# Feed-forward input tiles moved apart in a hybrid encoder layer: untouched tiles of 8 to 120 numbers between them

## The chip, the cores and the metric

The kernel runs on one core of a Trainium2 chip. The metric is the device time of one execution in microseconds. The engines are named as in the profile: PE is TensorE, DVE is VectorE, ACT is ScalarE, POOL is GpSimd, SP is the engine that issues most DMAs.

## The reference

One layer of an encoder, for two sequences of 1024 rows and width 1024 (`x_prompt` and `x_sample`), each with its own conditioning vector `c`. All numbers are float32.

```python
mod = jax.nn.silu(c) @ w_ada + b_ada                 # shift, scale, gate, twice
h = rmsnorm(x, g_mix) * (1.0 + sc1) + sh1
z = h @ w_in
y_mla = mla_group(q_lat, kv_lat, k_pe, ...)          # latent attention, 4 heads, softmax over 1024 keys
y_four = fourier_group(f_in, w_four)                 # 2-D Fourier mixing in 8 groups of 64
x = x + ga1 * (jnp.concatenate([y_mla, y_four], axis=-1) @ w_out)
h2 = rmsnorm(x, g_ffn) * (1.0 + sc2) + sh2
ffn = (jax.nn.silu(h2 @ w_gate) * (h2 @ w_up)) @ w_down      # inner width 2816
y = rmsnorm(x + ga2 * ffn, g_final)
```

## The kernel before

**Precision.** Each product of two float32 matrices is made of three matmuls. `split` (L63 to L65) cuts a tile into a high part (a cast by ACT, L64) and a low part (source minus high part, usually by DVE, L65). `mm3` (L79 to L82) then multiplies high by high (L80), high by low (L81) and low by high (L82) into the same PSUM bank. In `nc.tensor.matmul(out, weights, moving)` the first operand is loaded into the array 128 columns at a time (a weight load, PEld in the profile), and the second streams through, here mostly 512 columns of 4 bytes. While a matmul streams, the weights of the next are being loaded.

**Stages.** Projections and Fourier mixing come first, then attention, from about 300 to 715 us (`scores`, L1211 to L1223: per head and half of 256 rows five matmuls of 512 columns for each half of the keys; sequence 0 up to 505 us, then sequence 1), then from about 746 us the feed-forward part: gate/up of sequence 0, its down projection, gate/up of sequence 1, its down projection.

**Feed-forward, gate/up.** Both gate/up products use a scheme of the Strassen kind with seven products in place of eight, so the normalised input `h2` of a sequence is kept as seven combinations, numbered k = 0 to 6. Each is a pair of tiles: `Hk0` holds the high part and `Hk1` the low part, both `[128, 4, 512]` float32, 8192 bytes in each partition. `prep_h` loads and splits them. For each of 22 blocks of the inner width, seven weight combinations are split by `hl` into a pair `wh`, `wl` of `[128, 512]` tiles (eight buffers each), and `prod` runs, for chunk c of four:

```python
mm3(ps, wh[:, cs], wl[:, cs], H[k][0][:, c, :], H[k][1][:, c, :], first and c == 0, c == 3, not first)
```

So `wh` and `wl` are the weights here, an H tile is what streams, and `Hk0` streams twice where `Hk1` streams once.

**Down projection.** `prod2` multiplies `wh`, `wl` by `wh`, `wl`: both operands are from the same eight-buffer tiles. Its raw data arrives in X0 and X1. Only in the last product of sequence 1 do H tiles serve again, as holders of both operands (`held`, filled by `prep_last`).

**Memory.** Tiles come from stacked pools. Pool `p5` (`w`) takes its tiles from one end of the on-chip memory; the loop over 16 tags in front of `prep_h` reserves X0, X1 and the fourteen H tiles one behind the other by calling `quad(tag)`. Pool `p5b` (`w5`), with `wh`, `wl`, the 18 `val` buffers and some more, grows from the other end (`side="right"`), next to an unused tile of 104 numbers, `edge`, made at the start. Memory that a pool takes over from an earlier one is guarded by waits, tile by tile (`reuse_waits="tile"`): the first writer of a tile waits for the last users of whatever lay there.

**Order.** Instructions stand on each engine in the order in which the code records them, with small corrections by `issue_after` and `first`. Nothing in that order depends on addresses; only waits do.

Of the kernel before, what the change touches and what calls it, by code (L numbers as in the profile page):

```python
# [12 lines left out]
F32 = mybir.dt.float32  # L13
# [8 lines left out]
P = 128  # L22
# [32 lines left out]
def hybrid_encoder_kernel(ctx: ExitStack, tc: tile.TileContext, a: dict):  # L55
# [111 lines left out]
    with ExitStack() as st:  # L167
        p1b = st.enter_context(ExitStack())
        w2 = p1b.enter_context(tc.tile_pool(name="p1b", bufs=1, side="right", reuse_waits="tile"))
        w = st.enter_context(tc.tile_pool(name="p1", bufs=1, reuse_waits="tile"))  # L170
# [747 lines left out]
    with ExitStack() as st:  # L918
        early = st.enter_context(ExitStack())
        wa = early.enter_context(tc.tile_pool(name="p2a", bufs=1, reuse_waits="tile"))  # L920
        w = st.enter_context(tc.tile_pool(name="p2", bufs=1, side="right", reuse_waits="tile"))
# [283 lines left out]
    with ExitStack() as st:  # L1205
        w = st.enter_context(tc.tile_pool(name="p3", bufs=1, side="right", reuse_waits="tile"))
# [158 lines left out]
    with ExitStack() as st:  # L1365
        w = st.enter_context(tc.tile_pool(name="p5", bufs=1, reuse_waits="tile"))
# [6 lines left out]
        def quad(tag, dt=F32):  # L1373
            return w.tile([P, 4, 512], dt, tag=tag, name=tag, bufs=1)


        for tag in ("H20", "X0", "X1", "H21", "H30", "H31", "H00", "H41", "H01", "H50", "H51", "H10", "H11", "H40", "H60", "H61"):
            quad(tag)

        def prep_h(H, s, n):  # L1380
# [611 lines left out]
```

## Time and profile before

| | us |
|---|---|
| median of two runs | 2029.03 (2029.02 to 2029.04) |
| the profiled execution | 2027.96 |
| its span, first to last instruction | 2026.1 |
| PE busy in the span | 1978.9 |
| DVE, ACT, POOL busy | 1399.9, 891.0, 827.2 |

How such rows are read. A row of the groups names the line, the engine, the operation, the tiles (out<-in, buffer numbers left out), the shape and the count, then the busy time in us and the mean of one in ns, then the idle time ahead of them and what ended it. All H tiles are one name, `H`, there. A row of a source line gives the least, median and greatest duration, and the first and last start. A row of the timeline gives the start and the duration in us. Matmuls overlap: a duration of 389 ns with starts 227 ns apart is a full stream, and the distance of starts is what a matmul costs. A row of the stretches gives the busy time and, in brackets, the number of instructions of PE, PEld, DVE, ACT and POOL (only those that are there), then the granted clock of PE, the DMA share and GB/s.

### The profile page before, as it was taken

The numbers are of one execution on the slowest core, as the hardware profiler recorded it, in microseconds if no ns is written. First come the engines' busy times: TensorE is split into PE (matmuls) and PEld (weight loads), VectorE is DVE, ScalarE is ACT, GpSimd is POOL, SyncE is SP. The second block draws the span as 40 slices with busy tenths as digits, with TensorE's granted clock in tenths as the row PEclk, the third lists the DMA queues.
The fourth block names the chain that finished last, engine by engine and source line by source line (L and its number), as shares of the span: only waits on it lengthen the run. The fifth ranks groups of instructions, "written<-read, shape, count | busy, mean of one in ns | idle before, by whom it ended". The sixth has DMA issues, their size and how long they took to land.

```text
span 2026.1 us, 28369 instructions
## 1 busy us (share of the span) xinstructions
PE 1978.9 (98%) x9910; PEld 1640.5 (81%) x9910; DVE 1399.9 (69%) x2076; ACT 891.0 (44%) x1732; POOL 827.2 (41%) x972
## 2 busy tenths in 40 slices
PE   6899999999999999999999999999999999999998
PEld 3788778888888878888888888877888888888876
DVE  4567758666677779777777676778755655667685
ACT  2675435555565564333333365454333333336441
POOL 0664212111313237879779410333554454410142
PEclk9999999999999999999999999999999999999999
DMA  9696884434544475645645587665322322358662
GB/s 392 256 324 205 287 312 109 134 94 101 151 119 140 142 259 181 212 163 190 205 158 196 177 309 246 214 233 177 124 95 104 111 98 104 109 186 276 220 229 94
DMA packets 183037, 376.64 MB, mean 186 GB/s; under 512 B 17997, under 2 KB 57549, under 8 KB 179053
## 3 DMA queue, kind: packets, MB, share of 16 engines
q1 hardware_dynamic: 165548, 321.33, 46.3%
q0 software_dynamic: 17344, 53.49, 8.9%
q8 instruction: 78, 1.28, 0.3%
q14 instruction: 67, 0.54, 0.1%
HBM read 262.75 MB, written 120.39 MB: 189 GB/s over the span
## 4 chain that ended last, share of the span: by engine, by line
PE 54%; DVE 4%; DMA 2%; issue 1%; POOL 1%; ACT 1%; SPq 0%; DVEq 0%; ACTq 0%; POOLq 0%
PE bank L81 18%; PE bank L80 18%; PE bank L82 18%; DVE wl L65 2%; DVE val L140 1%; DMA draw<-s_d 1%; DMA draw<-t_d 1%; DVE val L1789 0%; ACT wh L64 0%; DVE val L137 0%; DMA X<-hc_d 0%; POOL val L140 0%; POOL rs_y L108 0%; DVE val L1778 0%; DVE val L1763 0%
## 5 line engine op out<-in xcount | busy, mean ns | idle before, releaser
L80 PE MATMUL bank<-H,wh 128*128 128x512 f32 x1232 | 480.0, 390 | 3.3 <-DVE val L140 1.3
L81 PE MATMUL bank<-H,wh 128*128 128x512 f32 x1232 | 479.5, 389 | 0.3 <-DVE H L65 0.3
L82 PE MATMUL bank<-H,wl 128*128 128x512 f32 x1232 | 479.3, 389 | 0.2 <-DVE wl L65 0.2
L80 PEld LDWEIGHTS bank<-H,wh 128*128 128x128 f32 x1232 | 231.2, 188 | 54.1 <-DVE val L1669 2.2
L82 PEld LDWEIGHTS bank<-H,wl 128*128 128x128 f32 x1232 | 231.2, 188 | 48.5 <-DVE wl L65 0.5
L81 PEld LDWEIGHTS bank<-H,wh 128*128 128x128 f32 x1232 | 231.2, 188 | 48.3 <-DVE H L65 0.6
L65 DVE TENSOR_TENSOR wl<-draw,wh 128x512 fp32r<-128x512 f32 x286 | 202.9, 744 | 85.2 <-ACT wh L64 84.4
L140 DVE TENSOR_TENSOR val<-bank,val 128x512 f32<-128x512 f32 x200 | 136.6, 689 | 154.0 <-PE bank L82 151.9
L64 ACT CAST wh<-draw 128x512 fp32r<-128x512 f32 x286 | 168.3, 620 | 157.8 <-PE bank L81 90.3
L140 POOL TENSOR_TENSOR val<-val 128x512 f32<-128x512 f32 x58 | 83.1, 1441 | 353.1 <-DVE val L1763 189.6
L81 PE MATMUL bank<-wl,wh 128*128 128x512 f32 x572 | 223.7, 391 | 3.4 <-DVE wl L65 3.4
L82 PE MATMUL bank<-wh,wl 128*128 128x512 f32 x572 | 222.7, 389 | 0.0
L80 PE MATMUL bank<-wh 128*128 128x512 f32 x572 | 222.6, 389 | 0.0
L64 ACT CAST wh<-rgu 128x512 fp32r<-128x512 f32 x172 | 107.1, 623 | 258.3 <-PE bank L81 201.0
L64 ACT CAST wh<-val 128x512 fp32r<-128x512 f32 x133 | 82.3, 622 | 259.0 <-PE bank L81 244.0
L65 DVE TENSOR_TENSOR wl<-rgu,wh 128x512 fp32r<-128x512 f32 x172 | 171.0, 994 | 3.8 <-ACT wh L64 3.8
L65 DVE TENSOR_TENSOR wl<-val,wh 128x512 fp32r<-128x512 f32 x133 | 126.1, 950 | 64.4 <-ACT wh L64 64.3
L137 POOL TENSOR_TENSOR val<-rgu 128x512 f32<-128x512 f32 x80 | 112.7, 1409 | 92.9 <-DMA rgu<-in_wgu_dram 89.2
L81 PEld LDWEIGHTS bank<-wl,wh 128*128 128x128 f32 x572 | 107.3, 188 | 28.7 <-DVE wl L65 6.7
L80 PEld LDWEIGHTS bank<-wh 128*128 128x128 f32 x572 | 107.4, 188 | 22.5
L82 PEld LDWEIGHTS bank<-wh,wl 128*128 128x128 f32 x572 | 107.4, 188 | 22.1
L1228 DVE TENSOR_REDUCE mx<-ps_s 128x1 f32<-128x1024 f32 x64 | 78.2, 1221 | 60.6 <-PE ps_s L1223 60.2
(385 smaller groups left out, 4052.4 us busy)
## 6 DMA issues: line engine op xcount, KB each, us to landing
rgu<-in_wgu_dram SPq DMA_DIRECT2D x86, 512.0 KB, 4.3
draw<-s_d SPq DMA_DIRECT2D x143, 256.0 KB, 3.8
s_d<-val POOLq DMA_DIRECT2D x88, 256.0 KB, 4.1
draw<-t_d SPq DMA_DIRECT2D x88, 256.0 KB, 4.2
s_d<-val SPq DMA_DIRECT2D x66, 256.0 KB, 2.6
draw<-in_w_down_dram SPq DMA_DIRECT2D x55, 256.0 KB, 4.6
wada<-in_w_ada_dram SPq DMA_DIRECT2D x11, 1024.0 KB, 10.5
xt<-in_x_dram SPq DMA_DIRECT2D x16, 512.0 KB, 10.2
```

The source lines that it names most:

```text
L64: here["a"] = nc.scalar.copy(hi, src).ins
L65: here["v"] = (eng or nc.vector).tensor_tensor(out=lo, in0=src, in1=rd(hi), op=ALU.subtract).ins
L80: nc.tensor.matmul(out, lh, rh, start=first, stop=False, skip_group_check=cont)
L81: nc.tensor.matmul(out, lh, rl, start=False, stop=False, skip_group_check=cont)
L82: here["t"] = nc.tensor.matmul(out, ll, rh, start=False, stop=last, skip_group_check=cont).ins
L137: return eng.tensor_tensor(out=out, in0=x, in1=y, op=ALU.subtract).ins
L140: eng.tensor_tensor(out=out, in0=x, in1=y, op=ALU.add)
L1228: nc.vector.tensor_reduce(out=mx, in_=ps, axis=AX.X, op=ALU.max)
```

## The change

Ahead of ten of the sixteen tiles an extra tile is reserved that nothing writes or reads. Its size is 8 to 120 float32 numbers in each partition.

```diff
+        apart = {"H20": 64, "H21": 64, "H30": 96, "H00": 72, "H41": 48, "H01": 80, "H50": 8, "H10": 16, "H40": 24, "H60": 120}
         for tag in ("H20", "X0", "X1", "H21", "H30", "H31", "H00", "H41", "H01", "H50", "H51", "H10", "H11", "H40", "H60", "H61"):
+            if tag in apart:
+                w.tile([P, apart[tag]], F32, name=f"apart{tag}")
             quad(tag)
```

The extra tiles take 592 numbers, 2368 bytes, in each partition. Every H tile and X0, X1 start later than before, by 256 to 2368 bytes. `wh`, `wl` and the rest of `p5b` stay where they were. In the two built programs these are the addresses; all `wh` and `wl` buffers start at 64 modulo 512, and a weight chunk of 128 columns is 512 bytes long:

| tiles | modulo 512 before | modulo 512 after | distance to `wh`, `wl` before | after |
|---|---|---|---|---|
| H00, H01 | 64 | 224 | 0 | 160 |
| H10, H11 | 64 | 320 | 0 | 256 |
| H20 | 64 | 320 | 0 | 256 |
| H21 | 64 | 64 | 0 | 0 |
| H30, H31 | 64 | 448 | 0 | 384 |
| H40, H41 | 64 | 416 | 0 | 352 |
| H50, H51 | 64 | 256 | 0 | 192 |
| H60, H61 | 64 | 384 | 0 | 320 |
| X0, X1 | 64 | 320 | 0 | 256 |

The instructions of all engines stay the same, in the same order. Some waits at the start of the pool differ, as a moved tile covers other memory of the stage before. On ACT this is the place where the last split of the attention output (`o0b`) is followed by the first splits of an H pair, H00 from its raw data in H20. A bracket names the counters that an instruction waits for: DMAHW and DMASW count transfers issued by SP and POOL, the others an engine's instructions. Before:

```order
L64 COPY pt_8112<-ppt 128x4x128 [waits PE_49] x2
L64 COPY o0b_7948<-gb 128x256 [waits PE_49]
L64 COPY H_8313<-H_8293 128x1024 [waits DMAHW1_49]
L64 COPY H_8313<-H_8293 128x1024 [waits DMAHW2_49]
L1175 ACTIVATE xn,ms_8198<-x_7977 128x1024 [waits DMAHW7_49,DVE_49]
```

After (lines behind the change stand three further down; the numbers in the names differ since more tiles are made ahead of them):

```order
L64 COPY pt_8112<-ppt 128x4x128 [waits PE_49] x2
L64 COPY o0b_7948<-gb 128x256 [waits PE_49]
L64 COPY H_8323<-H_8303 128x1024 [waits DMAHW4_49,DMAHW5_49,DMAHW3_49,DMAHW7_49,DMAHW1_49,Pool_49]
L64 COPY H_8323<-H_8303 128x1024 [waits DMAHW2_49]
L1175 ACTIVATE xn,ms_8198<-x_7977 128x1024 [waits DMAHW7_49,DVE_49]
```

The first split of H00 now waits, besides for its own data, for four earlier loads and for POOL: H00 has come to lie partly on tiles `hca` and `hcb` of the stage before. The DVE split behind it waited for that POOL instruction before the change too. The other differences of this kind are the loads of H21 and H30 on SP, and on ACT the second use of L1448, which writes into H41.

## The prediction

> **What bounds the kernel now.** First the page: its span, the share of TensorE, and the chain that ended last.
>
> ```profile
> span 2026.1 us, 28369 instructions
> PE 1978.9 (98%) x9910; PEld 1640.5 (81%) x9910; DVE 1399.9 (69%) x2076; ACT 891.0 (44%) x1732; POOL 827.2 (41%) x972
> PE 54%; DVE 4%; DMA 2%; issue 1%; POOL 1%; ACT 1%; SPq 0%; DVEq 0%; ACTq 0%; POOLq 0%
> PE bank L81 18%; PE bank L80 18%; PE bank L82 18%; DVE wl L65 2%; DVE val L140 1%; DMA draw<-s_d 1%; DMA draw<-t_d 1%; DVE val L1789 0%; ACT wh L64 0%; DVE val L137 0%; DMA X<-hc_d 0%; POOL val L140 0%; POOL rs_y L108 0%; DVE val L1778 0%; DVE val L1763 0%
> ```
>
> TensorE works in 98% of the span, and 54% of the span lies in the three lines of mm3 (L80 to L82). So I ask next how many of those matmuls read the tiles that the change moves (groups by line), and how densely they follow each other (the stretches, first for the instructions of H alone, then for all engines).
>
> ```profile
> L80 PE MATMUL bank<-H,wh 128*128 128x512 f32 x1232 | 480.0, 390 | 3.3 <-DVE val L140 1.3 <-DVE val L1669 0.8 <-ACT H L64 0.7
> L81 PE MATMUL bank<-H,wh 128*128 128x512 f32 x1232 | 479.5, 389 | 0.3 <-DVE H L65 0.3
> L82 PE MATMUL bank<-H,wl 128*128 128x512 f32 x1232 | 479.3, 389 | 0.2 <-DVE wl L65 0.2
> ...
> 1330.00:1806.00 476.00, 419.68 (x1848) 346.70 (x1848) 0.00 (x0) 0.53 (x1) 1.00 0.36 124
> ...
> 1320.00:1805.00 485.00, 481.32 (x2117) 396.41 (x2115) 314.16 (x405) 168.01 (x294) 219.04 (x216) 1.00 0.36 127
> ```
>
> 3 x 1232 = 3696 matmuls stream an H tile, 528 for each of the seven pairs. In the second gate/up stage 1848 of them fill 419.68 us, that is 227.1 ns from one start to the next, at a granted clock of 1.00. In that stretch TensorE is idle for 3.7 us of 485, while VectorE works for 314 us. **Whatever a matmul there takes longer, the kernel takes longer**; the other engines have slack.
>
> **What the change does to instructions.** It adds none, removes none and leaves their order on every engine as it was: the new tiles are never written or read. It does two things: it moves addresses, and with them a few waits for earlier users of the memory.
>
> **The waits.** The first ACT split of H00 now also waits for the POOL subtraction into hcb, four loads into hca and its own data; its old wait was the data alone. The second L1448 waits for the four hc_d stores as well. On SP the load of H21 waits for a later split of qa, the load of H30 for one matmul more.
>
> ```profile
> 692.20 1.62 POOL L137 TENSOR_TENSOR hcb<-hca,hcb 128x512 f32<-128x512 f32 x1
> 694.12 0.57 POOL L1282 DMA_DIRECT2D hc_d<-hcb  x1 [0.30 <-POOL hcb L137]
> ...
> L1282 POOL DMA_DIRECT2D hc_d<-hcb x4: 571/614/682, 622.4 to 694.1; - x4
> ...
> DMA to landing us min/median/max: 4.2/7.8/10.4
> ...
> 721.71 2.00 ACT L64 CAST H<-H 128x1024 fp32r<-128x1024 f32 x2
> ...
> 704.68 0.41 DVE L65 TENSOR_TENSOR qa<-gb,qa 128x256 fp32r<-128x256 f32 x1
> ...
> 715.29 0.98 SPq L1395 DMA_DIRECT2D H<-hc_d  x2
> ```
>
> The POOL operation ends at 693.8 us, the loads that it read are older, and the last store lands by 694.1 + 10.4 = 704.5 us. ACT starts that split at 721.71 and the second L1448 comes later still. The last qa split ends at 705.1, and SP issues the load at 715.29. Every new wait is over 10 us old when it is reached, except the single matmul, 0.23 us, in front of the H30 load; behind it on SP stand loads for splits some 10 us later. I take **0 us**, with 0 to 0.3 as ends. Were this cover gone, a split 10 us late would cost TensorE about that.
>
> **The addresses.** That is the real question: does a matmul care where its streamed tile lies against the weights being loaded beside it? Before, every H tile, wh and wl lie at 64 bytes modulo 512, so the distance is 0. After, it is 160 (H00, H01), 256 (H10, H11), 256 and 0 (H20, H21), 384 (H3x), 352 (H4x), 192 (H5x), 320 (H6x). The trace of before has a natural experiment on this. In attention, scores() runs the same five matmuls of 512 columns for both sequences; in the program as built the lat tiles of sequence 0 lie at 64 modulo 512, as qa and qp do (distance 0), those of sequence 1 at 0 (distance 448). Line L1222, first up to 505 us (sequence 0), then after (sequence 1), and one stretch of each from the timeline:
>
> ```profile
> L1222 PE MATMUL ps_s<-lat,qp x64: 389/389/400, 301.7 to 501.9; 128*128 128x512 f32 x64
> ...
> L1222 PE MATMUL ps_s<-lat,qp x64: 388/394/398, 505.5 to 713.2; 128*128 128x512 f32 x64
> ...
> 301.69 0.39 PE L1222 MATMUL ps_s<-lat,qp 128*128 128x512 f32 x1
> 303.96 0.39 PE L1222 MATMUL ps_s<-lat,qp 128*128 128x512 f32 x1
> ...
> 521.34 0.39 PE L1219 MATMUL ps_s<-lat,qa 128*128 128x512 f32 x1
> 523.66 0.28 PE L80 MATMUL gb<-wq_h,ql 128*128 128x256 f32 x1
> ```
>
> The median is 389 ns at distance 0 and 394 at 448. Ten matmuls from 301.69 to 303.96 make 227 ns each; ten from 521.34 to 523.66 make 232. **A distance of 448 costs 5 ns.** The Fourier output stage gives other distances at 512 columns: six matmuls on wm and B (distance 64), then six on wm and A (a mix of 32, 352, 416 and 480):
>
> ```profile
> 275.52 0.39 PE L80 MATMUL bank<-wm,B 128*128 128x512 f32 x1
> 276.91 0.39 PE L80 MATMUL bank<-wm,A 128*128 128x512 f32 x1
> 278.29 0.39 PE L1033 MATMUL bank<-wn,ny 128*128 128x512 f32 x1
> ```
>
> 1.39 us over six is 231.7 ns, 1.38 over six 230.0: 4.7 and 3.0 more than 227. Between this and the scores row I take 5 ns, since that row has the most samples in a steady stream, with 3.0 and 5.3 as ends.
>
> [...]
>
> Distance 256 has no steady row at 512 columns. The nearest are the 448-column matmuls on wz, three at 256 and then three at 0:
>
> ```profile
> 103.29 0.36 PE L80 MATMUL bank<-wz_h,eoh 128*128 128x448 f32 x1
> 103.90 0.36 PE L80 MATMUL bank<-wz_h,eoh 128*128 128x448 f32 x1
> 104.50 0.37 PE L80 MATMUL bank<-wz_h,eoh 128*128 128x448 f32 x1
> ```
>
> 203 ns against 200, so I take 3 ns for 256, with 0 (if the pattern repeats every 256 bytes) and 5.3 as ends.
>
> **The sum.** Five pairs at distances other than 0 and 256: 5 x 528 x 5 ns = 13.2 us. At 256 stand the whole pair H10/H11 (528) and two thirds of H20/H21 (352, as mm3 streams the first of a pair twice): 880 x 3 ns = 2.6 us. The 176 on H21 stay at 0. Together 15.8 us, all on TensorE and not hidden. Ends: 2640 x 3.0 = 7.9, and 3520 x 5.3 = 18.7. A slower TensorE may let the waits of 3.7 us a stage shrink; I count nothing for that. X0 and X1 move as well, but TensorE does not read them; their readers ACT, DVE and POOL work beside it. If VectorE lost its slack there, its L65 would have to slow by half first (485 over 314).
>
> The profiled execution took 2027.96 us, 1.9 more than its span and 1.07 less than the median of 2029.03. With 15.8 it would be 2043.8; against the median, **2045 us, 0.8% longer**.
>
> **Rivals.** *Distance does not matter.* What sequence 1 shows would then be due to its neighbours. For it speaks that some matmuls at distance 0 in attention also come slowly: three on wv and o0b from 729.57, then three more.
>
> ```profile
> 729.57 0.40 PE L80 MATMUL gb<-wv,o0b 128*128 128x512 f32 x1
> 730.28 0.39 PE L80 MATMUL gb<-wv,o0b 128*128 128x512 f32 x1
> 730.97 0.39 PE L80 MATMUL gb<-wv,o0b 128*128 128x512 f32 x1
> ```
>
> That is 237 and 230 ns. Against it: these stand right behind 256-column matmuls, as the scores of both sequences do, and only the stream at distance 0 settles at 227. It gives 2029, within 1.5. [...]
>
> *Faster, off distance 0.* At 256 columns distance 0 is the slow one: pt against ckv stands at 480, ql against wq_h at 0.
>
> ```profile
> 520.04 0.28 PE L81 MATMUL gb<-pt,ckv 128*128 128x256 f32 x1
> 521.22 0.28 PE L82 MATMUL gb<-pt,ckv 128*128 128x256 f32 x1
> ...
> 524.37 0.28 PE L80 MATMUL gb<-ql,wq_h 128*128 128x256 f32 x1
> 524.97 0.28 PE L82 MATMUL gb<-ql,wq_l 128*128 128x256 f32 x1
> ```
>
> Ten in 1.18 us are 118 ns, five in 0.60 are 120. If a weight load hit the stream less often off distance 0, and 512 columns followed these rows, each of the 3520 moved matmuls would gain 2 to 4 ns: 7 to 14 us, 2015 to 2022. It decides as soon as most of the seven distances fall below 227 ns. Against it, none of the three 512-column stretches above does. [...]
>
> *A higher price.* Distances 160 and 192 were not seen at 512 columns, and in the feed-forward stage three more engines read and write. With the slow stretch of 237 as the price, 3520 x 10 = 35 us: 2064.
>
> That the tiles are not set apart at all is excluded by the addresses of the built program.
>
> **Chances.** Forecast 0.76, no effect 0.09, faster 0.07, higher price 0.08. The range 2035 to 2057 takes in the forecast with its ends (2037 to 2048) and the lower half of the higher price, 0.80 together. A change of 2%, 40.6 us, which is about what a measurement of this kernel can tell from no change, needs 11.5 ns on each of the 3520: slower by that 0.02, faster 0.01, within 0.97.
>
> **What would show it.** The stretch of the second gate/up stage should hold fewer than 2117 matmuls in 485 us, and the 1848 on H should take about 428 us (231 ns); the medians of L80 to L82 on H should rise from 389 to 393 or so, those of bank<-wh,wl (down projection, untouched) stay at 389. Everything before 746 us should look as before, the ACT split at 721.7 with it. The forecast is wrong if H stays at 389, or if new idle time ahead of the first H matmuls carries the difference.

## The result and the profile after

| | before | after |
|---|---|---|
| median, us | 2029.03 (2029.02 to 2029.04) | 2049.16 (2048.46 to 2049.87) |
| the profiled execution | 2027.96 | 2048.46 |
| its span | 2026.1 | 2046.6 |

The ratio is 1.0087, with an interval of 1.0058 to 1.0116: slower by 0.9%, less than 2%, and clear of no change; the 2% that the prediction takes as about what can be told here is too coarse. The two spans differ by 20.5 us. The page, the line groups of TensorE, the stretch of the second gate/up stage (H alone, then all engines; the columns are as before) and the starts of the H matmuls show where they went.

```profile
span 2046.6 us, 28372 instructions
PE 2002.1 (98%) x9910; PEld 1643.0 (80%) x9910; DVE 1399.9 (68%) x2076; ACT 890.9 (44%) x1732; POOL 827.2 (40%) x972
...
L80 PE MATMUL bank<-H,wh 128*128 128x512 f32 x1232 | 486.1, 395 | 3.1 <-DVE val L1672 1.1
L82 PE MATMUL bank<-H,wl 128*128 128x512 f32 x1232 | 485.6, 394 | 0.2 <-DVE wl L65 0.2
L81 PE MATMUL bank<-H,wh 128*128 128x512 f32 x1232 | 484.7, 393 | 0.3 <-DVE H L65 0.3
...
L82 PE MATMUL bank<-wh,wl 128*128 128x512 f32 x572 | 222.7, 389 | 0.0
...
740.00:1240.00 500.00, 430.34 (x1848) 1.00 0.59 203
...
1330.00:1826.00 496.00, 429.11 (x1848) 1.00 0.36 125
...
1330.00:1826.00 496.00, 492.25 (x2123) 397.97 (x2123) 319.90 (x406) 168.83 (x296) 219.81 (x217) 1.00 0.36 125
```

The mean of one H matmul rose from 389 or 390 ns to 393 to 395; a matmul of the down projection still takes 389. DVE, ACT and POOL are busy as long as before. The 1848 H matmuls of the second gate/up stage fill 429.11 us, where they filled 419.68. In the first they fill 430.34; before it was this row:

```profile
740.00:1240.00 500.00, 421.44 (x1848) 1.00 0.61 208
```

So H takes 9.4 + 8.9 = 18.3 us more. About 2.2 us remain, and as much is lost ahead of everything that the change touches. Start of the first scores matmul, before and after:

```profile
301.01 0.39 PE L1219 MATMUL ps_s<-lat,qa 128*128 128x512 f32 x1
...
303.29 0.39 PE L1219 MATMUL ps_s<-lat,qa 128*128 128x512 f32 x1
```

The code up to there is the same, and in the traces of e1 to e7, where it is the same too, that matmul starts anywhere from 301.18 to 305.73 us. Executions of the kernel before on the chips of the experiments range from 2027.19 to 2034.43 us. So I count this as the spread between executions. The 132 matmuls of the last product, whose two operands both lie in H tiles, start 230.1 ns apart where they started 226.7 ns apart before (means of the traces), 0.4 us together; about as much is saved elsewhere on the way. The new waits cost nothing: the ACT split that got one starts right behind the split of `o0b`, without idle time of its own, 2.2 us later on the clock like all its surroundings.

```profile
723.60 0.37 ACT L64 CAST o0b<-gb 128x256 fp32r<-128x256 f32 x1 [1.60 <-PE gb L82]
723.87 2.00 ACT L64 CAST H<-H 128x1024 fp32r<-128x1024 f32 x2
```

What each pair costs can be read from a single block of the inner width. It is 84 matmuls, twelve for each pair in the order k = 0, 5, 1, 6, 4, 3, 2. These are the first rows of two successive blocks before, and then the first row of each pair of a block after, with the seventh row of the last pair (1610.11) and the first of the next block at the end (timeline of TensorE).

```profile
1577.20 0.39 PE L80 MATMUL bank<-H,wh 128*128 128x512 f32 x1
1596.24 0.39 PE L80 MATMUL bank<-H,wh 128*128 128x512 f32 x1
```

```profile
1592.00 0.40 PE L80 MATMUL bank<-H,wh 128*128 128x512 f32 x1
1594.80 0.39 PE L80 MATMUL bank<-H,wh 128*128 128x512 f32 x1
1597.60 0.39 PE L80 MATMUL bank<-H,wh 128*128 128x512 f32 x1
1600.36 0.40 PE L80 MATMUL bank<-H,wh 128*128 128x512 f32 x1
1603.12 0.39 PE L80 MATMUL bank<-H,wh 128*128 128x512 f32 x1
1605.93 0.39 PE L80 MATMUL bank<-H,wh 128*128 128x512 f32 x1
1608.73 0.39 PE L80 MATMUL bank<-H,wh 128*128 128x512 f32 x1
1610.11 0.39 PE L80 MATMUL bank<-H,wh 128*128 128x512 f32 x1
1611.47 0.40 PE L80 MATMUL bank<-H,wh 128*128 128x512 f32 x1
```

Before, 19.04 us over seven pairs of twelve: 226.7 ns a matmul. After, 19.47: 2.80 us (233 ns) for k = 0 at 160, 2.80 for k = 5 at 192, 2.76 (230) for k = 1 at 256, 2.76 for k = 6 at 320, 2.81 (234) for k = 4 at 352, 2.80 for k = 3 at 384, 2.74 (228) for k = 2 at 256 and 0.

The last pair is not even within itself. Its first six matmuls take 1.38 us, 230.0 ns each, and its last six 1.36 us, 226.7 ns each. Over all 44 blocks the means are 230.8 and 226.8 ns. Four of those last six stream H20, at distance 256. So a loss that begins in one pair, here the one at 384 ahead, reaches into the next and then wears off, and the mixture of 256 and 0 that is left runs at the full rate. In the pair k = 1, at 256 throughout and behind the pair at 192, the last two matmuls are at 227 ns (medians over the blocks) and those ahead of them mostly are not.

### The profile page after: what moved, and what is told of

Read it like the earlier page. It is cut to its first block, busy times and chain, and to the rows that moved or that the text cites. A ratio compares the mean times of both kernels' runs of the same rounds, so it can differ in the third digit from the quotient of the medians.

```text
span 2046.6 us, 28372 instructions
## 1 busy us (share of the span) xinstructions
PE 2002.1 (98%) x9910; PEld 1643.0 (80%) x9910; DVE 1399.9 (68%) x2076; ACT 890.9 (44%) x1732; POOL 827.2 (40%) x972
## 4 chain that ended last, share of the span: by engine, by line
PE 56%; DVE 3%; DMA 2%; issue 1%; POOL 1%; ACT 1%; SPq 0%; DVEq 0%; ACTq 0%; POOLq 0%
PE bank L81 19%; PE bank L82 19%; PE bank L80 19%; DVE wl L65 1%; DMA draw<-t_d 1%; DMA draw<-s_d 1%; DVE val L140 0%; ACT wh L64 0%; POOL val L140 0%; DVE val L1792 0%; DMA X<-hc_d 0%; DVE val L1766 0%; POOL rs_y L108 0%; SPq L1751 0%; DVE val L137 0%
## 5 line engine op out<-in xcount | busy, mean ns | idle before, releaser
L80 PE MATMUL bank<-H,wh 128*128 128x512 f32 x1232 | 486.1, 395 | 3.1 <-DVE val L1672 1.1
L82 PE MATMUL bank<-H,wl 128*128 128x512 f32 x1232 | 485.6, 394 | 0.2 <-DVE wl L65 0.2
L81 PE MATMUL bank<-H,wh 128*128 128x512 f32 x1232 | 484.7, 393 | 0.3 <-DVE H L65 0.3
L80 PEld LDWEIGHTS bank<-H,wh 128*128 128x128 f32 x1232 | 231.4, 188 | 59.0 <-DVE val L140 1.9
L82 PEld LDWEIGHTS bank<-H,wl 128*128 128x128 f32 x1232 | 231.3, 188 | 54.8 <-DVE wl L65 0.5
L80 PE MATMUL bank<-wh 128*128 128x512 f32 x572 | 222.7, 389 | 0.0
L82 PE MATMUL bank<-wh,wl 128*128 128x512 f32 x572 | 222.7, 389 | 0.0
L65 DVE TENSOR_TENSOR wl<-val,wh 128x512 fp32r<-128x512 f32 x133 | 137.7, 1037 | 69.5 <-ACT wh L64 69.4
L65 DVE TENSOR_TENSOR wl<-rgu,wh 128x512 fp32r<-128x512 f32 x172 | 161.9, 941 | 4.5 <-ACT wh L64 4.4
L80 PEld LDWEIGHTS bank<-wh 128*128 128x128 f32 x572 | 107.4, 188 | 22.9 <-ACT wh L64 0.3
L82 PEld LDWEIGHTS bank<-wh,wl 128*128 128x128 f32 x572 | 107.4, 188 | 21.9
```

The source lines that it names most:

```text
L65: here["v"] = (eng or nc.vector).tensor_tensor(out=lo, in0=src, in1=rd(hi), op=ALU.subtract).ins
L80: nc.tensor.matmul(out, lh, rh, start=first, stop=False, skip_group_check=cont)
L81: nc.tensor.matmul(out, lh, rl, start=False, stop=False, skip_group_check=cont)
L82: here["t"] = nc.tensor.matmul(out, ll, rh, start=False, stop=last, skip_group_check=cont).ins
```

## The experiments

Each kernel here is the kernel before with one edit; none leaves any work out. Times of e1 to e4 stand against a median of 2029.32 us for the kernel before on the same chip, those of e5 to e8 against 2029.82.

**e1: the tiles moved by whole multiples of 512 bytes.**

```diff
+        apart = {"H20": 128, "H21": 128, "H30": 128, "H00": 128, "H41": 128, "H01": 128, "H50": 128, "H10": 128, "H40": 128, "H60": 128}
...
+            if tag in apart:
+                w.tile([P, apart[tag]], F32, name=f"apart{tag}")
```

> Ten untouched tiles as in the change, but each of 128 numbers (512 bytes), so that the H tiles move by up to 5120 bytes while every distance to wh and wl stays 0 modulo 512. If the distance modulo 512 is what costs (theory), the matmuls on H start every 227 ns as before, their medians stay at 389 ns, and the time is 2029 us within the 2 us by which the first 300 us differ between executions. If it was the shifting itself, the waits at the start of the pool or the larger pool (rival), the time is near 2049 us.

Measured: 2030.05 us, ratio 0.9997 (0.9987 to 1.0008). The stretch that holds the H matmuls of the second gate/up stage, and one line of it:

```profile
1300.00:1830.00 530.00, 419.67 (x1848) 1.00 0.40 138
...
L80 PE MATMUL bank<-H,wh x596: 389/389/497, 1399.7 to 1806.8; 128*128 128x512 f32 x199
```

419.67 us against 419.68 before. Untouched tiles between the H tiles, 5120 bytes of them, cost nothing as long as the distance stays 0.

**e2: the weights moved instead of the inputs.** One untouched tile of 40 numbers beside `wl` puts all `wh` and `wl` 160 bytes lower (and two tiles that TensorE does not read); H and X tiles stay.

```diff
             l = w5.tile([P, 512], F32R, tag="wl", name="wl", bufs=8)
+            if "shift" not in S:
+                S["shift"] = w5.tile([P, 40], F32, name="shift")
```

> No tile between the H tiles; instead wh and wl alone lie 160 bytes lower, so that all seven pairs stand at distance 160, and X0, X1 and all H tiles stay where they were before. Theory, distance between streamed tile and weights: all 3696 matmuls on H cost as the pair H00/H01 did in the change (about 234 ns, 7 more than before), 26 us in all, 2055 us; the down projection, where both operands come from wh and wl (distance 0 still), keeps its median of 389 ns. Rival, the address of the streamed tile alone modulo 512: H stays at 389 ns, and the 1716 matmuls of the down projection become slower by about 7 ns, 12 us, 2041 us.

Measured: 2055.67 us, ratio 1.0127 (1.0111 to 1.0143). The same stretch, then L80 on H and, from 1270 us on, L80 in the down projection:

```profile
1300.00:1830.00 530.00, 432.56 (x1845) 1.00 0.38 129
...
L80 PE MATMUL bank<-H,wh x611: 392/397/505, 1400.3 to 1830.2; 128*128 128x512 f32 x153
...
L80 PE MATMUL bank<-wh x103: 388/389/389, 1270.0 to 1339.4; 128*128 128x512 f32 x103
```

432.56 us over 1845 are 234.5 ns each. The H tiles lie where they lay, and their matmuls are slow; in the down projection both operands moved together, and nothing changed. That is the distance, not the address of what streams.

**e3: both moved, to the same remainder.** The first H tile 160 bytes higher, all behind it with it; `wh` and `wl` 352 bytes lower, 224 modulo 512 on both sides.

```diff
+        apart = {"H20": 40}
...
+            if "shift" not in S:
+                S["shift"] = w5.tile([P, 88], F32, name="shift")
```

> All H tiles 160 bytes higher and wh, wl 352 bytes lower, so that both lie at 224 modulo 512 and the distance is 0 again. Theory (distance): H at 227 ns, 389 ns median, 2029 us within 2. Rival (an address other than 64 modulo 512 is slow by itself): H at about 234 ns, 2055 us, and the down projection slower too.

Measured: 2029.69 us, ratio 0.9999 (0.9989 to 1.0009).

```profile
1300.00:1830.00 530.00, 419.65 (x1848) 1.00 0.40 138
```

Remainder 224 is as good as 64 if both have it: 419.65 us against 419.68. e1 to e3 together show the cause: the distance between the streamed tile and the weight tiles, with 227.1 ns a matmul at 0 in e1 and e3 and 234.5 at 160 in e2. Modulo 512 it was 0 wherever nothing was lost; whether 256 would do as well comes under e5 and e6.

**e4: only `wh` moved.** To tell whether the weights in use or those being loaded count.

```diff
             if "gf" not in S:
+                w5.tile([P, 40], F32, name="shift")
                 S["gf"] = w5.tile([P, D], F32, name="gf")
```

> Only wh lies 160 bytes lower, wl and H stay. Which distance counts, that to the weights being used or that to the weights being loaded for the next matmul? In mm3 L80 uses wh and loads wh, L81 uses wh and loads wl, L82 uses wl and loads wh. If the loaded weights count (theory): on H, L80 and L82 slow (start to next start about 234 ns), L81 at 227; in the down projection L80 and L81 stream wh and wl while their own kind is loaded, L82 streams wh while wh is loaded, all distance 0, so nothing changes there; 2464 x 7 ns = 17 us, 2046 us. If the weights in use count (rival): L80 and L81 slow, L82 at 227, and in the down projection L81 and L82 slow as well, 1144 x 7 ns = 8 us more, 2054 us. If one disturbed matmul of three is enough to slow all three: 2055 us.

Measured: 2049.69 us, ratio 1.0098 (1.0071 to 1.0126); its profiled execution had lost some microseconds ahead of the first H matmul, so the lines count here. On H, then in the down projection:

```profile
L80 PE MATMUL bank<-H,wh x616: 391/392/501, 1401.6 to 1828.5; 128*128 128x512 f32 x154
L81 PE MATMUL bank<-H,wh x616: 389/392/396, 1401.8 to 1828.8; 128*128 128x512 f32 x154
L82 PE MATMUL bank<-H,wl x616: 391/394/397, 1402.0 to 1829.0; 128*128 128x512 f32 x154
...
L80 PE MATMUL bank<-wh x102: 389/393/397, 1269.7 to 1339.9; 128*128 128x512 f32 x102
L81 PE MATMUL bank<-wl,wh x101: 393/397/400, 1269.9 to 1339.5; 128*128 128x512 f32 x101
L82 PE MATMUL bank<-wh,wl x101: 390/393/395, 1270.1 to 1339.7; 128*128 128x512 f32 x101
```

Neither answer holds by itself. On H all three lines rose about equally; from start to start they take 229.6, 230.0 and 230.4 ns (means of the trace, gaps over 260 ns left out). In the down projection the distance to the weights being loaded is 0 for all three, and still all three are slower (230.4, 234.4 and 230.9 ns from start to start), so loading alone doesn't decide. (In the trace of before, the load for the next matmul mostly starts 3 or 4 ns after a matmul does and takes 188 ns, so it is the next one's weights that are being loaded.) The third case, that one broken matmul slows all, fits the form, but the price is 3 ns on H, half of the 7 that it was given.

**e7: only the low tile of each pair moved**, to 160; the high one stays at 0.

```diff
+        apart = {"H21": 40, "H30": 88, "H31": 40, "H00": 88, "H41": 40, "H50": 88, "H51": 40, "H10": 88, "H11": 40, "H40": 88, "H61": 40}
...
+            if tag in apart:
+                w.tile([P, apart[tag]], F32, name=f"apart{tag}")
```

> Only the low tile of each pair (Hk1, streamed by L81) stands at distance 160; the high tile (Hk0, streamed by L80 and L82) stays at 0. If each matmul pays for its own distance: L81 at about 234 ns, L80 and L82 at 227; 1232 x 7 = 9 us, 2038 us. If a broken stream slows its neighbours too (rival, suggested by H21 in the change, which stood at 0 between two matmuls at 256 and cost 230): L80 and L82 rise as well, all three near 230, 3696 x 3 = 11 us, 2040 us. The total does not tell them apart, the time from start to start by line does.

Measured: 2049.47 us, ratio 1.0095 (1.0076 to 1.0113), 9 us and more above both cases.

```profile
L80 PE MATMUL bank<-H,wh x609: 397/397/501, 1399.7 to 1825.6; 128*128 128x512 f32 x153
L81 PE MATMUL bank<-H,wh x609: 389/391/394, 1399.9 to 1825.8; 128*128 128x512 f32 x153
L82 PE MATMUL bank<-H,wl x609: 390/397/397, 1400.2 to 1826.0; 128*128 128x512 f32 x153
```

The matmuls that stream the tile at 0 (L80, L82) show the higher medians, the one at 160 the lower; from start to start the means are 234.4, 230.9 and 231.3 ns. One matmul in three at another distance costs about three quarters of what all three cost in e2: 5.5 ns a matmul against 7.6, and 19.7 us against 26.4. So a matmul does not pay for its own distance alone: one at 0 is slow beside neighbours at 160. And the steady 226.7 ns comes back only after some matmuls: in the last pair of the change the first six take 230.8 ns, the last six 226.8.

**e5 and e6: fourteen more distances.** e5 has pads as in the change, of other sizes. In e6 five pairs start a few numbers into larger tiles, which puts them at 4, 8, 16, 240 and 508 bytes.

```diff
+        apart = {"H20": 8, "H30": 8, "H00": 8, "H41": 8, "H01": 120, "H50": 32, "H10": 16, "H40": 88, "H60": 72}
```

```diff
+        within = {"H00": 1, "H41": 2, "H01": 1, "H50": 4, "H51": 4, "H10": 7, "H11": 7, "H40": 2, "H60": 4, "H61": 4}
...
-            return w.tile([P, 4, 512], dt, tag=tag, name=tag, bufs=1)
+            if tag not in within:
+                return w.tile([P, 4, 512], dt, tag=tag, name=tag, bufs=1)
+            t = w.tile([P, 2056], dt, tag=tag, name=tag, bufs=1)
+            return t[:, within[tag] : within[tag] + 2048].rearrange("p (a b) -> p a b", a=4)
...
+        apart = {"H20": 112, "H30": 8, "H00": 8, "H41": 120, "H01": 120, "H50": 120, "H51": 120, "H10": 112, "H11": 120, "H60": 48, "H61": 120}
```

> The seven pairs at seven distances that the change did not have, the high and low tile of a pair at the same one: H2x 32, H3x 64, H0x 96, H4x 128, H5x 224, H1x 288, H6x 416. Theory (only a whole multiple of 512 lets the stream settle at 227 ns): each pair costs 3 to 7 ns more a matmul, as the pairs of the change did, about 5 on average, 3696 x 5 = 18 us, 2047 us. Rival (the pattern repeats at 64 or 128 bytes, and the price depends on the remainder): H3x and H4x, or H4x alone, stay at 227 ns.

> Seven more distances, four of them smaller than 32 bytes: H0x 4, H4x 8, H5x 16, H1x 508, H6x 240, H3x 480, H2x 448 (the tiles H0x, H1x, H4x, H5x, H6x are 32 bytes larger for it, and what is used starts some numbers into them). Theory that any remainder breaks the settled stream: all seven at 230 to 234 ns, 2047 us. [...]

Measured: 2051.37 us, ratio 1.0104 (1.0086 to 1.0123), and 2053.83 us, ratio 1.0116 (1.0098 to 1.0135). One block of e5, then one of e6, first rows of the pairs in the order k = 0, 5, 1, 6, 4, 3, 2 and of the next block:

```profile
1595.00 0.39 PE L80 MATMUL bank<-H,wh 128*128 128x512 f32 x1
1597.79 0.40 PE L80 MATMUL bank<-H,wh 128*128 128x512 f32 x1
1600.58 0.40 PE L80 MATMUL bank<-H,wh 128*128 128x512 f32 x1
1603.38 0.40 PE L80 MATMUL bank<-H,wh 128*128 128x512 f32 x1
1606.19 0.39 PE L80 MATMUL bank<-H,wh 128*128 128x512 f32 x1
1608.97 0.40 PE L80 MATMUL bank<-H,wh 128*128 128x512 f32 x1
1611.73 0.39 PE L80 MATMUL bank<-H,wh 128*128 128x512 f32 x1
1614.52 0.39 PE L80 MATMUL bank<-H,wh 128*128 128x512 f32 x1
```

```profile
1595.05 0.40 PE L80 MATMUL bank<-H,wh 128*128 128x512 f32 x1
1597.92 0.39 PE L80 MATMUL bank<-H,wh 128*128 128x512 f32 x1
1600.69 0.39 PE L80 MATMUL bank<-H,wh 128*128 128x512 f32 x1
1603.45 0.39 PE L80 MATMUL bank<-H,wh 128*128 128x512 f32 x1
1606.28 0.40 PE L80 MATMUL bank<-H,wh 128*128 128x512 f32 x1
1609.09 0.39 PE L80 MATMUL bank<-H,wh 128*128 128x512 f32 x1
1611.88 0.39 PE L80 MATMUL bank<-H,wh 128*128 128x512 f32 x1
1614.67 0.40 PE L80 MATMUL bank<-H,wh 128*128 128x512 f32 x1
```

Each difference over twelve, with those of the change, gives ns per matmul by distance (a hundredth of a us over twelve is 0.8 ns):

| distance | 0 | 4 | 8 | 16 | 32 | 64 | 96 | 128 | 160 | 192 | 224 |
|---|---|---|---|---|---|---|---|---|---|---|---|
| ns | 226.7 | 239 | 234 | 231 | 232 | 230 | 232 | 232 | 233 | 233 | 232 |

| distance | 240 | 256 | 288 | 320 | 352 | 384 | 416 | 448 | 480 | 508 |
|---|---|---|---|---|---|---|---|---|---|---|
| ns | 236 | 230 | 233 | 230 | 234 | 233 | 234 | 232 | 232 | 230 |

Over all blocks the means are within 1 ns of these. They are prices of a pair in its place, with what the pair ahead of it left over, so they can't be read as prices of a distance alone: no pair as a whole stood at 0 among the others, and the 230 at 256 seems to be mostly such a rest, by the last pair of the change.

The last six matmuls of a pair are freer of it. At 64 they take 229.0 ns and at 384 233.3 (means over the blocks), so the free distances repeat neither every 64 nor every 128 bytes. A period of 256 is not excluded, and more speaks for it than against it: the last six of the mixture of 256 and 0 take 226.8 ns, and distances 256 apart mostly end alike, 64 and 320 at 229.0 and 228.9, 192 and 448 both at 233.3; 128 and 384 do not, 231.0 and 233.3. No run has all tiles at 256, which would settle it. The dearest distance is 4 bytes, one number: 239 ns, and 234 at 8, against 231 at 16.

**e8: the same cause where the trace of before had shown it first**, in attention. The untouched tile ahead of `pt0` grows from 8 to 120 numbers, which brings the lat tiles of sequence 1 to distance 0.

```diff
-                    w.tile([P, 8], F32, name="gap0")
+                    w.tile([P, 120], F32, name="gap0")
```

> The kernel before, with the untouched tile ahead of pt0 in attention made 480 bytes instead of 32, so that the lat tiles of sequence 1 (and the tile p) move from 0 to 64 modulo 512, to distance 0 from qa and qp; nothing in the feed-forward part moves. Theory: L1219 to L1223 of sequence 1 fall from a median of 394 to 389 ns as in sequence 0, 320 matmuls x 5 ns = 1.6 us less, 2027.4 us where TensorE bounds that stretch. If the difference between the sequences had another cause (rival): median 394, 2029 us. The tile p, whose parts are the weights of the transposes into ppt, moves against ident from a distance of 128 to 64 as well; if that costs as much as it gains, the medians tell.

Measured: 2028.52 us, ratio 0.9995 (0.9986 to 1.0004), the same within its interval. L1222 of sequence 1, and the stretch of that sequence for all engines, in e8 and then before:

```profile
L1222 PE MATMUL ps_s<-lat,qp x64: 389/389/398, 505.8 to 714.0; 128*128 128x512 f32 x64
...
505.00:713.00 208.00, 204.42 (x1295) 180.85 (x1294) 148.84 (x271) 116.41 (x246) 57.02 (x82) 1.00 0.47 137
```

```profile
505.00:713.00 208.00, 205.53 (x1297) 181.30 (x1296) 148.84 (x271) 115.91 (x246) 57.74 (x82) 1.00 0.47 136
```

The median fell from 394 to 389 as expected, and TensorE is busy 1.1 us less in a window of the same length. But sequence 1 is no shorter: from the first L1222 to the last it takes 208.2 us, before 207.7. The waits of the transposes (L1251) for VectorE's softmax (L1235) between 505 and 714 us went from 0.3 us in all to 1.3. That is one trace of each, so it is likely and not shown that the shorter matmuls end in longer waits there. The 1.6 us hoped for are also smaller than what the interval can tell. As a faster version it is not shown.

## Why the prediction was right

Forecast 2045 us, measured 2049.16, inside 2035 to 2057. By its steps:

- *TensorE is the bound in gate/up, so what a matmul costs there is paid in full.* Right. H took 18.3 us more, the rest of TensorE's work, but for 0.4 us in the last product, none, and no other engine came to bound. TensorE's idle time in the second stage did not shrink either, 3.68 us before and 3.75 after.
- *The new waits cost nothing.* Right; the split on ACT starts without idle time. It starts 2.2 us later than the prediction's signs had it, but so does all around it.
- *5 ns for a distance other than 0 and 256.* Right in kind, too small in size. The row taken, scores at 448, is 232 ns in e6 too. But the change's five distances cost 233, 233, 230, 234 and 233: on average 6.0 above 226.7, 15.8 us over 2640 matmuls in place of 13.2. Distances 160 and 192, for which there was no row, cost 233 like most others.
- *3 ns for 256.* Right in size, 230, 3.3 more on the pair k = 1, but by luck. The rows that it was taken from, 203 against 200 ns, differ by one hundredth of a us over three matmuls, the last digit that is shown. Over all matmuls of that product the trace of before has 204.0 ns at 256 and 204.0 at 0 (means, longer gaps left out). And in the change the matmuls at 256 run at the full rate at the end of k = 2. By this, what these two pairs paid came at least in large part over from the pairs ahead of them, at 192 and 384. The lower end of that term, 0 if the pattern repeats every 256 bytes, is nearer to what the trace shows.
- *The 176 matmuls on H21 stay at 0 cost.* Wrong in its reasoning. Their mean from start to start was 230.0 ns although they stood at distance 0, while the H20 matmuls around them at 256 came to 228. Place decides, not distance: the H21 matmuls at the second and fifth place of the pair took 235.5 and 230.7 ns, those at the eighth and eleventh 227.0 and 226.6 (means over the blocks). For the pair the sum came out as forecast, 2.74 us for twelve, and that is luck: no term of the prediction has a loss that passes from one pair to the next.
- *The sum of 15.8 us.* 18.3 on H, 2.5 more, nearly all of it from the five distances. The 0.4 us of the last product, where H tiles hold both operands, had no term. Most of what is left in the profiled execution arose ahead of 301 us and was in no term; it is the spread of the first stage.

The rival *distance does not matter* is out by e2 with e3: the same H tiles at the same addresses run at 234.5 ns against 227 when only the weights move, and back at 227 when both do. The rival *faster off distance 0* is out by the 20 distances of the table, none below 230. *A higher price*, 237 ns as the mean of a pair, exists among the distances tried at 4 only, which the change does not have.

## What to carry to other kernels

Where TensorE is the bound and streams 512 float32 columns against weights loaded beside them, look at the addresses of both tiles in a partition modulo 512 and make them equal for all tiles of the stream: here that is 226.7 ns against 230 to 239, up to 5%, and a single tile in three with another remainder (160) costs about three quarters as much as all (19.7 us in e7, 26.4 in e2). Equal remainders modulo 256 may be enough; that was not run on its own. A small unused tile is enough to do or undo it: 160 bytes beside `wl` cost 26.4 us in e2, and with equal remainders on both sides e3 was back at 2029.69 us. So a new tile whose size is no multiple of 512 bytes, declared for quite another purpose, can slow matmuls that it has nothing to do with. In the attention part the same correction showed in the median of L1222, 389 ns in place of 394, and not in the time: ratio 0.9995 (0.9986 to 1.0004) in e8.

## What the runs showed of the hardware that was not expected

- A distance of one number, 4 bytes, is the worst of those tried, 239 ns, 12 more than at 0; 508, which is 4 bytes to the other side, is among the mildest at 230.
- The price is not the single matmul's. In e7 the two lines at distance 0 had medians of 397 ns, the one at 160 of 391. In e4 every distance to the weights being loaded was 0 in the down projection, and all three lines rose, to 393, 397 and 393.
- The loss outlasts what caused it. Behind a pair at 384, the first six matmuls of the next pair take 230.8 ns and only the last six 226.8, whichever of its two tiles they stream.
- Why a distance costs time, and whether the free distances lie 512 or 256 bytes apart, no run here shows. The distance to the weights being loaded can't be all: it was 0 throughout in the down projection of e4. Nor can the distance to the weights in use: it is 0 for all matmuls of the last product after the change, which take 230.1 ns in place of 226.7. In both, the stream moves between tiles of different remainders, and no run tells that jump from the distance to the weights.
